# Hybrid encoder layer step: two more projection blocks taken from unscaled rows, layer norm's factor and shift applied behind the spatial products, and an instruction order that counts the shared PSUM banks

## The chip, the cores and the metric

The kernel runs on one NeuronCore of a Trainium2 chip, in fp32. The metric is the device time of one execution in microseconds (us), as a median of runs. Engines are named as in the profile: PE (matrix products), PEld (its weight loads), DVE, ACT and POOL (elementwise work), SP (which issues most DMAs). A bank is one of the eight PSUM banks into which PE writes.

## What is computed

One layer of a streaming encoder on 576 tokens: 64 of a running stream and 512 of a new one, width 1024. Cut to what matters:

```python
h   = rms_norm(x) * g
p   = h @ w_in                    # columns r|k|v|lora w,a,g | u|gv | gate_A | gate_B
o_A = rwkv7(p[r,k,v,lora])        # token shift, decay, delta rule state per head
vn  = layer_norm(p[gv])           # (gv - mean) * rstd * ln_v_g + ln_v_b
z   = einsum('gts,bnsgc->bntgc', w_spatial * tril, vn) + b_spatial
o_B = p[u] * z
m   = sigmoid(p[gate_A]) * (o_A @ w_proj_a) + sigmoid(p[gate_B]) * (o_B @ w_proj_b)
x   = x + rms_norm(m @ w_o)
x   = x + rms_norm(swiglu(rms_norm(x)))
```

The normalised `vn` of the 64 running tokens is an output too. The token shift is `p + (p_prev - p) * mu`. The recurrence is done in chunks of 64 tokens: per chunk a 64 x 64 triangular inverse, then a short chain of states over nine chunks.

## The kernel before

**Layout.** Channels lie on partitions and the 576 tokens along the free dimension, in two halves of 288. A projection *block* is 128 output channels: for eight input tiles, two halves and three terms, 48 matmuls of 128 x 288. Three terms, because every fp32 operand is split into a rounded part and a rest (`hi`, `lo`), and hi*hi, hi*lo and lo*hi are added. A weight block is loaded (`wraw`, L280, two buffers), split by ACT (`whi`, L287) and POOL (`wlo`, two halves, L290) into three buffers.

**Start.** x is loaded and multiplied by the norm's gain; its split is `u0..u7` (the unscaled rows: the factor 1/rms of each token is missing). From these come the two lora blocks (`pfw`, `pfg`), then k and r of the first head pair (`pk`, L546 to L560), which are kept in `st` tiles. The token factors `rs0` are ready meanwhile, and `Shifted(scale=True)` (L465) multiplies such a block by them before the token shift (L468 to L473). The scaled and split rows `h0..h7` (L583, L331, L332) follow; all later blocks use them (`pj`). Then the early pool `xpool` is closed and its space is given to the pools of the head pairs.

**Weave.** The order of PE's instructions is written out by a planner, class `Weave`: PE executes exactly in that order. There are streams, written as Python generators, and background blocks:

- `elementwise` of each of eight head pairs: z (lora products), n (norms of k), am (products within chunks; twice two banks, then two), tb and tr (transposes), tv (transposes of v), wv, bo;
- `inverse` of each pair: m1, m2, mp, mu, d, e and c, y, in this order, behind the small inverse on DVE (X, M, with DMAs through `d_inv`);
- `chain` (states, pc, then py), `finish` (group norm, to, g, store to `d_oa`);
- behind the pairs: layer norm (`ln_all`), spatial products z (`ob_all`), loading of `d_oa` (`oa_all`), norms.

A stream hands control back with a number, after which it may go on, or with an event and a number. The numbers are the estimates in `LAT`: n2 from k to n, tb between transposes, e0 ahead of e and so on; `name@p` holds for pair p alone. The planner keeps a clock `now`, raised by each matmul's estimated time. When no stream may go on it takes three more matmuls of the current block. If the estimate is short, PE stands at that instruction and waits; if it is long, the stream goes on late and blocks run in between.

Blocks wait in a list: first `F0` gate blocks, then for each pair its k, r, v (which need the event A of the pair before; pair 0 has only v here) and `FILL[p]` more gate and u blocks (`spill`, stored to `d_ga`, `d_gb`, `d_u`), then the four gv quarters, then the three blocks that are left. A block whose need isn't there yet is passed over for a later one.

**Banks.** During the pairs four banks with tag `a` are shared by all streams (`ps1`), three serve blocks, one the state chain. They are given in turn. The planner doesn't know of them: PE waits at a matmul whose bank hasn't been read out.

**Other engines.** The orders of DVE, ACT, POOL and SP are set at build time by a scheduler with its own estimates, in priority of the program's order, and are fixed too.

**Layer norm.** Per group of rows (one of 64, four of 128 tokens): statistics, then ACT applies mean and 1/sigma (L1099), POOL multiplies by the gain and DVE adds the shift, each in two halves of 512 (L1102, L1103). Gain and shift lie in slots 5 and 6, broadcast to 128 partitions by DMA (L1017). In `ob_all`, eight groups g of 128 channels are multiplied by the masked `wsT` (name z, L1129), and the bias is added on DVE (L1132, L1133).

Of the kernel before, what the change touches and what calls it, by code (L numbers as in the profile page):

```python
# [5 lines left out]
F32 = mybir.dt.float32  # L6
# [6 lines left out]
P = 128  # L13
# [24 lines left out]
FILL = (1, 0, 2, 6, 3, 3, 1, 2)  # L38
LAT = {
# [4 lines left out]

# [37 lines left out]
def host_layout(a):  # L82
# [49 lines left out]
class Weave:  # L132
# [89 lines left out]
def layer(tc, I, O):  # L222
# [27 lines left out]
    ps1 = lambda name: psum.tile([P, 512], F32, tag="a", bufs=nb["a"], name=name)  # L250
# [278 lines left out]
    with tc.manual_schedule(engines={mybir.EngineType.PE}):  # L529
# [103 lines left out]
    def elementwise(E):  # L633
# [38 lines left out]
        s = ps1("n2")[:, 0:10].rearrange("p (j h) -> p j h", h=2)  # L672
# [34 lines left out]
        banks = lambda: [ps1("am").rearrange("p (j t) -> p j t", t=P) for _ in range(2)]  # L707
# [20 lines left out]
        yield LAT["am"]  # L728
        pm = banks()
# [729 lines left out]
```

## Time and profile before

| | us |
|---|---|
| median of 3 runs (lowest, highest) | 1274.91 (1273.36, 1278.71) |
| the profiled execution | 1273.24 |
| its span, first to last instruction | 1271.5 |
| PE busy | 1195.4 (94%) |
| DVE, ACT, POOL busy | 583.3, 466.2, 630.5 |
| mean granted PE clock | 0.968 |

The span is what the profiler saw between the first and the last instruction. Busy time of PE overstates its work a little, since matmuls overlap. A time in square brackets behind an instruction is how long its engine stood idle ahead of it, with the instruction that ended the wait. "DMA issue" rows give the size and the time from issue to landing. The granted clock is the share of full speed that the chip allowed PE.

### The profile page before, as it was taken

The page shows a single profiled execution, that of the slowest core. Times are in us where ns is not written, and L with a number is a line of the kernel's source. Part 1 is how long each engine was busy: PE and PEld are TensorE (multiplying, and loading weights), DVE is VectorE, ACT ScalarE, POOL GpSimd, SP SyncE. Part 2 cuts the span into 40 slices and gives each one's busy share as a digit, 9 for nine tenths or more (in the row PEclk, how much of TensorE's full clock was granted, in tenths as well). Part 3 has the DMA queues.
Part 4 walks back from the last instruction along what each step waited for, and adds up shares of the span by engine and source line. Part 5 has one row for each costly group of instructions (what it writes and reads, how often), then busy time and mean ns, then how long its engine had stood idle before and what let it go on. Part 6 is the DMA issues. An engine that isn't in the chain of part 4 may idle for free.

```text
span 1271.5 us, 29927 instructions
## 1 busy us (share of the span) xinstructions
PE 1195.4 (94%) x12922; PEld 1162.5 (91%) x12922; DVE 583.3 (46%) x1077; ACT 466.2 (37%) x887; POOL 630.5 (50%) x492
## 2 busy tenths in 40 slices
PE   7889999999999989999879999989999999999997
PEld 6789888888898889899879999989999999999997
DVE  5965576663656647562741542464333333310003
ACT  5634343535253544443431233452222222222220
POOL 6554253533445344542663654366565656544442
PEclk8898899899899999999889999989999999999998
DMA  5212222223131313132554543223222222242222
GB/s 178 81 58 75 58 80 61 76 69 103 41 105 56 86 57 100 52 112 71 157 161 130 179 138 117 69 108 90 82 84 84 84 84 82 85 158 82 84 76 75
DMA packets 68404, 118.56 MB, mean 93 GB/s; under 512 B 30832, under 2 KB 36208, under 8 KB 68272
## 3 DMA queue, kind: packets, MB, share of 16 engines
q1 hardware_dynamic: 68128, 116.58, 30.3%
q8 instruction: 101, 1.65, 0.6%
q14 instruction: 31, 0.25, 0.1%
q10 hardware_dynamic: 144, 0.07, 0.0%
HBM read 100.35 MB, written 16.28 MB: 92 GB/s over the span
## 4 chain that ended last, share of the span: by engine, by line
PE 68%; DVE 15%; ACT 5%; POOL 4%; issue 4%; DMA 3%; SPq 1%; DVEq 0%; POOLq 0%; ACTq 0%
PE fg L271 20%; PE po L271 14%; PE pj L271 11%; PE pb L271 4%; PE pa L271 4%; PE gv L271 3%; POOL wlo L290 2%; DVE X L828 2%; PE am L271 1%; DVE Xt L825 1%; PE fp L271 1%; SPq L833 1%; PE z L271 1%; PE pc L271 1%; DVE L L650 1%
## 5 line engine op out<-in xcount | busy, mean ns | idle before, releaser
L290 POOL TENSOR_TENSOR wlo<-raw,whi 128x512 fp32r<-128x512 f32 (+1 forms) x288 | 406.5, 1434 | 372.4 <-ACT whi L287 352.5
L287 ACT ACTIVATE whi<-raw 128x1024 fp32r<-128x1024 f32 x144 | 150.2, 1046 | 283.9 <-PE fg L271 172.2
L1209 DVE TENSOR_TENSOR rs<-rs,nsq 128x288 f32<-128x288 f32 (+2 forms) x12 | 9.0, 754 | 104.7 <-ACT nsq L1208 104.7
L1277 DVE TENSOR_TENSOR ft<-ft,fg 128x288 f32<-128x288 f32 x40 | 16.4, 451 | 67.1 <-PE fg L271 65.5
L1271 DVE TENSOR_TENSOR fg<-fg,rs 128x288 f32<-128x288 f32 x40 | 16.4, 453 | 62.3 <-PE fg L271 62.2
L828 DVE TENSOR_TENSOR X<-X,Xt 80x15 f32<-80x15 f32 (+7 forms) x120 | 42.4, 353 | 3.4
L825 DVE TENSOR_TENSOR Xt<-X,M 80x15 f32<-80x15 f32 (+7 forms) x120 | 37.6, 314 | 8.7 <-DMA M<-d_inv 5.4
L976 POOL TENSOR_TENSOR gm<-gm,mhalf 128x10 f32<-128x10 f32 x8 | 16.2, 2023 | 42.8 <-DVE gm L975 42.8
L1274 DVE SCALAR_TENSOR_TENSOR ft<-ft,fg 128x576 f32<-128x576 f32 (+1 forms) x24 | 28.4, 1183 | 19.3 <-ACT ft L1273 19.3
L740 POOL TENSOR_TENSOR BK<-BK,EL 128x576 f32<-128x576 f32 x16 | 18.7, 1171 | 36.1 <-PE am L271 36.1
L1275 POOL TENSOR_TENSOR ft<-ft,rs 128x576 f32<-128x576 f32 (+1 forms) x24 | 31.8, 1326 | 7.1 <-DVE ft L1274 7.1
L271 PE MATMUL pj<-h0h,wlo 128*128 128x288 f32 x92 | 28.2, 307 | 5.7 <-POOL wlo L290 5.7
L836 DVE STREAM_TRANSPOSE IT<-IV 128x640 f32<-128x640 f32 x16 | 13.5, 841 | 43.9 <-DMA IV<-d_inv 31.1
L668 POOL TENSOR_TENSOR aq<-aq,k 128x576 f32<-128x576 f32 x8 | 12.8, 1604 | 39.4 <-DVE k L473 27.8
L271 PE MATMUL pj<-h0h,whi 128*128 128x288 f32 x92 | 29.8, 324 | 2.3 <-ACT whi L287 2.3
L271 PE MATMUL pj<-h4l,whi 128*128 128x288 f32 x92 | 28.0, 305 | 3.5 <-DVE h4l L332 3.5
L271 PE MATMUL pj<-h3h,whi 128*128 128x288 f32 x92 | 29.8, 324 | 0.0
L271 PE MATMUL pj<-h2h,whi 128*128 128x288 f32 x92 | 29.7, 323 | 0.0
L271 PE MATMUL pj<-h1h,whi 128*128 128x288 f32 x92 | 29.6, 321 | 0.0
L271 PE MATMUL pj<-h4h,whi 128*128 128x288 f32 x92 | 29.4, 319 | 0.0
L271 PE MATMUL pj<-h7h,whi 128*128 128x288 f32 x92 | 29.3, 319 | 0.0
L271 PE MATMUL pj<-h5h,whi 128*128 128x288 f32 x92 | 29.0, 316 | 0.0
(1194 smaller groups left out, 4309.4 us busy)
## 6 DMA issues: line engine op xcount, KB each, us to landing
raw<-in_w_in SPq DMA_DIRECT2D x50, 512.0 KB, 3.7
raw<-in_w_gate SPq DMA_DIRECT2D x22, 512.0 KB, 3.6
raw<-in_w_up SPq DMA_DIRECT2D x22, 512.0 KB, 3.6
raw<-in_w_down SPq DMA_DIRECT2D x16, 512.0 KB, 3.5
raw<-in_w_gv SPq DMA_DIRECT2D x8, 512.0 KB, 3.6
raw<-in_w_proj_a SPq DMA_DIRECT2D x8, 512.0 KB, 4.0
raw<-in_w_proj_b SPq DMA_DIRECT2D x8, 512.0 KB, 3.6
raw<-in_w_o SPq DMA_DIRECT2D x8, 512.0 KB, 3.6
```

The costliest lines, as they stand in the source:

```text
L271: return pe.matmul(out, lhsT, rhs, **kw)
L287: keep(act.activation(hi[:, :cols], raw[:, :cols], ACT.Copy))
L290: keep(pool.tensor_tensor(lo[:, c0:c1], raw[:, c0:c1], f(hi[:, c0:c1]), ALU.subtract))
L740: pool.tensor_tensor(by_chunk(BK[:, x, :]), by_chunk(BK[:, x, :]), EL[:, :, 64:65].broadcast_to([P, NCH, 64]), ALU.mult)
L825: ins = dve.tensor_tensor(t3, X[:, 0:r, s:s + 1].broadcast_to([NU, r, w]), M[:, s:s + 1, s + 1:SB].broadcast_to([NU, r, w]), ALU.mult)
L828: dve.tensor_tensor(X[:, 0:r, s + 1:SB], X[:, 0:r, s + 1:SB], t3, ALU.add)
L836: turn = lambda: dve.transpose(IT.rearrange("p c t -> p (c t)"), IV.rearrange("p c t -> p (c t)"))
L976: pool.tensor_tensor(m, m, mhalf, ALU.pow)
L1271: keep(dve.tensor_tensor(g[:, HS[h]], pg, rs2[:, HS[h]], ALU.mult))
L1274: keep(dve.scalar_tensor_tensor(t[:, ts], t[:, ts], 1.0, g[:, ts], ALU.add, ALU.mult))
L1275: pool.tensor_tensor(t[:, ts], t[:, ts], rs2[:, ts], ALU.mult)
L1277: dve.tensor_tensor(t[:, HS[h]], t[:, HS[h]], pu, ALU.mult)
```

## The change

1. **Start.** Behind k and r of pair 0, its v and the first gate_A block are also computed from the unscaled rows. v waits in an `st` tile (now three) and is scaled with the others. The gate block is multiplied by `rs0` on DVE, goes through Tanh on ACT, and is stored from a tile of `xpool`. Both blocks leave the weave's list, and `FILL` of pair 3 falls from 6 to 5.
2. **Order.** `Weave` counts the four shared banks: a request gives the time for which it holds the bank (`take`), and a stream that needs n banks hands control back until n are free by that count (`free(n)`). Every `ps1` of the pairs gets such a pair of lines; not all are shown. Many estimates in `LAT` change, e0 counts from d and not from the values, and AB is transposed last of three.
3. **Layer norm.** Gain and shift are applied to the 64 running tokens only. For the other four groups the gain, constant along a channel, is multiplied behind the spatial product, and the shift becomes `ln_b[c] * sum_s(w[t,s]) + b_spatial[t]`: two products of ones with `wsT` and eight DVE operations compute this once, into slot 5.

```diff
-FILL = (1, 0, 2, 6, 3, 3, 1, 2)
+FILL = (1, 0, 2, 5, 3, 3, 1, 2)
 LAT = {
-    "z0": 5.4, "z": 0.85, "n2": 4.9, "n2t": 0.4, "am0": 3.7, "am": 1.6, "tb0": 3.5, "tb": 0.8, "tv0": 4.6, "tv": 1.3, "bo0": 3.5, "bo": 0.4,
-    "last": 0.4, "ln": 3.5, "oa": 3.9, "oaj": 0.15, "z1": 18.0, "zz": 1.5, "rs": 2.15, "rb": 2.8, "f": 1.1, "f0": 1.0, "sq": 0.44,
-    "M": 5.5, "U": 20.0, "m1": 2.3, "m2": 2.4, "mp": 3.3, "mu": 2.0, "d0": 2.2, "e0": 2.3, "y0": 3.5,
-    "ch0": 2.6, "S": 1.5, "y": 0.5, "gn1": 4.0, "gn2": 6.0, "to": 3.5, "to1": 0.45, "g": 1.8,
-
-    "am0@0": 6.4, "am0@1": 5.6, "n2@0": 1.4, "tb0@1": 2.9, "M@0": 3.4,
+    "z0": 5.4, "z": 0.85, "n2": 6.2, "n2t": 0.4, "am0": 3.7, "am": 2.0, "tb0": 3.5, "tb": 1.3, "tv0": 5.2, "tv": 1.3, "bo0": 3.5, "bo": 0.4,
+    "last": 0.4, "ln": 3.5, "oa": 3.9, "oaj": 1.2, "z1": 15.0, "zs": 3.0, "zz": 1.5, "rs": 2.15, "rb": 2.8, "f": 1.1, "f0": 1.0, "sq": 0.44,
+    "M": 5.5, "U": 20.3, "m1": 2.3, "m2": 2.4, "mp": 4.2, "mu": 2.0, "d0": 2.2, "e0": 3.1, "y0": 3.5,
+    "ch0": 3.4, "S": 1.6, "y": 0.5, "gn1": 4.0, "gn2": 6.0, "to": 3.5, "to1": 0.45, "g": 1.8,
+
+    "am0@0": 6.4, "am0@1": 5.6, "n2@0": 4.2, "n2@1": 7.2, "n2@3": 7.2, "tb0@1": 3.5, "M@0": 3.4,
 }
...
+    def take(self, hold):
+
+        self.banks.sort()
+        self.banks.pop(0)
+        self.banks.append(self.now + hold)
+
+    def free(self, n=1):
+
+        while sorted(self.banks)[n - 1] > self.now:
+            yield sorted(self.banks)[n - 1] - self.now
...
-    ps1 = lambda name: psum.tile([P, 512], F32, tag="a", bufs=nb["a"], name=name)
+    def ps1(name, hold=0.0):
+        clk.take(hold)
+        return psum.tile([P, 512], F32, tag="a", bufs=nb["a"], name=name)
...
-        kr = []
-        for h in range(4):
...
+        raw0 = {}
+        for nm, b in (("k", BLK_K), ("r", BLK_R), ("v", BLK_V), (None, BLK_GA)):
+            w = wf[2] if nm == "k" else wblock(I["w_in"][b])
+            st = xp.tile([P, T], F32, name="st0") if nm is None else wp.tile([P, T], F32, tag="st", bufs=3, name="st")
+            for h in range(2):
+                ps = pk if (nm, h) == ("k", 0) else [psd("pk")[:, 0:HALF]] * 2
+                for k in range(2 if (nm, h) == ("k", 0) else 0, KD):
+                    mm(ps, w, uh, ul, k, KD, halves=(h,))
+                if (nm, h) == (None, 1):
+                    clk.prepare()
+                if nm is None:
+                    dve.tensor_tensor(st[:, HS[h]], ps[0], rs0[:, HS[h]], ALU.mult)
+                    act.activation(st[:, HS[h]], st[:, HS[h]], ACT.Tanh, scale=0.5)
+                else:
+                    act.activation(st[:, HS[h]], ps[0], ACT.Copy)
+            if nm is None:
+                sp.dma_start(d_ga[0], st)
+            raw0[nm] = st
...
-        s = ps1("n2")[:, 0:10].rearrange("p (j h) -> p j h", h=2)
+        yield from clk.free()
+        s = ps1("n2", 1.6)[:, 0:10].rearrange("p (j h) -> p j h", h=2)
...
-        banks = lambda: [ps1("am").rearrange("p (j t) -> p j t", t=P) for _ in range(2)]
+        banks = lambda: [ps1("am", 3.0).rearrange("p (j t) -> p j t", t=P) for _ in range(2)]
+        yield from clk.free(4)
         pm = banks()
...
-        rest = ps1("tr").rearrange("p (j v) -> p j v", v=P)
-        for i, (dst, src) in enumerate(((AB, BK[:, 0, :]), (At, AR[:, 0, :]), (Kt, BK[:, 1, :]))):
-            pt = ps1("tb").rearrange("p (j v) -> p j v", v=P)
+        yield from clk.free(2)
+        rest = ps1("tr", 5.0).rearrange("p (j v) -> p j v", v=P)
+        for i, (dst, src) in enumerate(((At, AR[:, 0, :]), (Kt, BK[:, 1, :]), (AB, BK[:, 0, :]))):
+            yield from clk.free()
+            pt = ps1("tb", 1.5).rearrange("p (j v) -> p j v", v=P)
...
-        pp = [ps1("d").rearrange("p (u t) -> p u t", t=P) for _ in range(3)]
+        yield from clk.free(3)
+        pp = [ps1("d", 2.8).rearrange("p (u t) -> p u t", t=P) for _ in range(3)]
...
-        yield (("values", hp_), LAT["e0"])
+        yield LAT["e0"]
+        yield (("values", hp_), 0.0)
...
-        pe_ = [ps1("e").rearrange("p (j a t) -> p j a t", a=2, t=64) for _ in range(2)]
-        pq = [ps1("c") for _ in range(2)]
+        yield from clk.free(4)
+        pe_ = [ps1("e", 4.0).rearrange("p (j a t) -> p j a t", a=2, t=64) for _ in range(2)]
+        pq = [ps1("c", 4.2) for _ in range(2)]
...
-        py = [ps1("y").rearrange("p (u v) -> p u v", v=HD) for _ in range(3)]
+        yield from clk.free(3)
+        py = [ps1("y", 3.2).rearrange("p (u v) -> p u v", v=HD) for _ in range(3)]
...
-            sp.dma_start(R["ln"][i], I["rows"][i:i + 1, :].broadcast_to([P, D]))
+            sp.dma_start(R["ln"][i][0:64], I["rows"][i:i + 1, :].broadcast_to([64, D]))
...
-            for i in range(2):
-                cs = slice(i * 512, (i + 1) * 512)
-                pool.tensor_tensor(vn[0:n, cs], vn[0:n, cs], gain[0:n, cs], ALU.mult)
-                dve.tensor_tensor(vn[0:n, cs], vn[0:n, cs], shift[0:n, cs], ALU.add)
             if n == 64:
+                for i in range(2):
+                    cs = slice(i * 512, (i + 1) * 512)
+                    pool.tensor_tensor(vn[0:n, cs], vn[0:n, cs], gain[0:n, cs], ALU.mult)
+                    dve.tensor_tensor(vn[0:n, cs], vn[0:n, cs], shift[0:n, cs], ALU.add)
                 sp.dma_start(O["vn_s"], vn[0:64])
...
+        pb = R["ln"][0]
+        for i in range(2):
+            ps = psum.tile([P, 512], F32, tag="h", bufs=6, name="zs")
+            mmul(ps, one.broadcast_to([P, P]), R["wsT"][:, i * 512:(i + 1) * 512], start=True, stop=True)
+            for g in range(4 * i, 4 * i + 4):
+                gs = slice(g * P, (g + 1) * P)
+                dve.scalar_tensor_tensor(pb[:, gs], ps[:, (g % 4) * P:(g % 4 + 1) * P], V("ln_b", g), R["bias"][:, gs], ALU.mult, ALU.add)
+        yield LAT["zs"]
...
-            dve.tensor_tensor(zb[:, 64:T].rearrange("p (c t) -> p c t", t=P), pz[1].rearrange("p (c t) -> p c t", t=P),
-                              bs.unsqueeze(1).broadcast_to([P, 4, P]), ALU.add)
+            dve.scalar_tensor_tensor(zb[:, 64:T].rearrange("p (c t) -> p c t", t=P), pz[1].rearrange("p (c t) -> p c t", t=P), V("ln_g", g),
+                                     pb[:, gs].unsqueeze(1).broadcast_to([P, 4, P]), ALU.mult, ALU.add)
...
-        for nm, b, x_ in (("k", BLK_K, kr[0]), ("r", BLK_R, kr[1])):
+        for nm, b in (("k", BLK_K), ("r", BLK_R), ("v", BLK_V)):
             take = Shifted(b, nm, scale=True)
-            EV[0][nm] = [take(h, x_[:, HS[h]]) for h in range(2)][1]
-        clk.signal("k", 0)
-        clk.signal("r", 0)
+            EV[0][nm] = [take(h, raw0[nm][:, HS[h]]) for h in range(2)][1]
+            clk.signal(nm, 0)
```

More of the change, by code (lines that the diff above doesn't have):

```diff
@@ L769, in elementwise @@
         v = E["v"]
-        pvs = [ps1("tv").rearrange("p (j v) -> p j v", v=P) for _ in range(2)]
+        yield from clk.free(2)
+        pvs = [ps1("tv", 1.6).rearrange("p (j v) -> p j v", v=P) for _ in range(2)]
         for j in range(5):
@@ L781, in elementwise @@
         WV = rp.tile([P, 10, HD], F32, tag="WV", name="WV")
-        pw = [ps1("wv").rearrange("p (u v) -> p u v", v=HD) for _ in range(2)]
+        yield from clk.free(2)
+        pw = [ps1("wv", 2.4).rearrange("p (u v) -> p u v", v=HD) for _ in range(2)]
         for c, j, half_ in PLACES:
@@ L801, in elementwise @@
         for hs in HS:
-            sb = ps1("bo")
+            yield from clk.free()
+            sb = ps1("bo", 1.2)
             mmul(sb[:, 0:HALF], bonesr, rkh[:, hs], start=True, stop=False)
@@ L842, in inverse @@
         yield lat("m1", hp_)
-        pp = ps1("m1")[:, 0:10 * SB].rearrange("p (c t) -> p c t", t=SB)
+        yield from clk.free()
+        pp = ps1("m1", 1.8)[:, 0:10 * SB].rearrange("p (c t) -> p c t", t=SB)
         for u in range(10):
@@ L848, in inverse @@
         yield lat("m2", hp_)
-        pp = ps1("m2")[:, 0:10 * SB].rearrange("p (c t) -> p c t", t=SB)
+        yield from clk.free()
+        pp = ps1("m2", 2.2)[:, 0:10 * SB].rearrange("p (c t) -> p c t", t=SB)
         for u in range(10):
@@ L858, in inverse @@
         yield lat("mp", hp_)
-        pp = ps1("mp")[:, 0:320].rearrange("p (c t) -> p c t", t=32)
+        yield from clk.free()
+        pp = ps1("mp", 1.9)[:, 0:320].rearrange("p (c t) -> p c t", t=32)
         for u in range(10):
@@ L865, in inverse @@
         yield lat("mu", hp_)
-        pp = ps1("mu")[:, 0:320].rearrange("p (c t) -> p c t", t=32)
+        yield from clk.free()
+        pp = ps1("mu", 1.9)[:, 0:320].rearrange("p (c t) -> p c t", t=32)
         for u in range(10):
@@ L952, in chain @@
         Y = E["Y"]
-        py = [ps1("py")[:, 0:320].rearrange("p (j v) -> p j v", v=HD) for _ in range(2)]
+        yield from clk.free(2)
+        py = [ps1("py", 2.2)[:, 0:320].rearrange("p (j v) -> p j v", v=HD) for _ in range(2)]
         for c, j, half_ in PLACES2:
@@ L982, in finish @@
         for js, t0, t1 in (((0, 2, 1, 3), 0, START2[4]), ((4,), START2[4], T)):
-            pt = ps1("to")
+            yield from clk.free()
+            pt = ps1("to", 1.4)
             for j in js:
@@ L990, in finish @@
         for hs in HS:
-            ps = ps1("g")
+            yield from clk.free()
+            ps = ps1("g", 1.4)
             for n, (w, xx) in enumerate(((lh, dgh), (lh, dgl), (ll, dgh))):
```

35 lines of the change are left out of this document (13 added, 22 removed).

## The prediction

> **What bounds the kernel now.** I read the page's busy shares and 40 slices first, then a table by stage, then the PE timeline with its waits.
>
> ```profile
> PE 1195.4 (94%) x12922; PEld 1162.5 (91%) x12922; DVE 583.3 (46%) x1077; ACT 466.2 (37%) x887; POOL 630.5 (50%) x492
> ...
> PE   7889999999999989999879999989999999999997
> ...
> PEclk8898899899899999999889999989999999999998
> ```
>
> PE is busy 94% of 1271.5 us; no other engine passes half. Its losses lie in the left half, and there the granted clock dips too. So the question is how many of PE's lost microseconds the change gives back. By stage (columns: us, then busy time and count of PE, PEld, DVE, ACT, POOL, granted clock, DMA):
>
> ```profile
> 42.40:76.40 34.00, 25.26 (x149) 23.66 (x147) 27.12 (x25) 17.89 (x37) 23.02 (x18) 0.85 0.21 70
> 76.40:552.80 476.40, 443.40 (x6918) 420.84 (x6916) 285.75 (x627) 210.92 (x481) 215.64 (x171) 0.96 0.26 74
> 552.80:603.50 50.70, 49.95 (x840) 48.32 (x839) 16.19 (x41) 17.22 (x38) 14.17 (x11) 1.00 0.29 88
> 603.50:660.00 56.50, 46.03 (x332) 44.41 (x332) 37.76 (x52) 22.07 (x35) 38.20 (x27) 0.88 0.49 152
> 660.00:723.00 63.00, 62.56 (x463) 60.49 (x464) 18.86 (x37) 12.96 (x16) 32.80 (x24) 1.00 0.48 141
> 723.00:1271.50 548.50, 535.23 (x4017) 532.83 (x4016) 168.38 (x264) 159.83 (x238) 283.50 (x215) 0.99 0.31 96
> 975.00:1000.00 25.00, 25.00 (x191) 25.00 (x190) 8.00 (x13) 6.96 (x8) 14.62 (x11) 1.00 0.28 85
> ```
>
> The last row is PE unhindered: 25.00/191 = 0.131 us for a matmul, so 6.3 us for a 48-matmul block. Three stages lose time: the start of the weave (8.7 us idle, clock 0.85), the eight head pairs (33.0 us idle, clock 0.96: 4% of 476.4 = 19 us withheld) and the layer norm (10.5 us idle, clock 0.88: 12% of 56.5 = 6.8 us withheld). What follows 723 is not touched.
>
> PE need not be the bound of the pairs merely because it is busy: they hang on a chain (inverse, then state). These rows tell:
>
> ```profile
> 143.29 1.66 PE y L271 x75
> ...
> 536.34 1.66 PE y L271 x75
> ...
> 589.09 1.66 PE y L271 x75
> ```
>
> From y of the first pair to y of the last is 445.8 us, 63.7 a pair. The last interval, with no later pair's elementwise work beside it, took 52.8: that is the chain's own length. So a pair is some 11 us longer than its chain, and fill blocks on PE set it. After the last pair's state PE still owes projection work:
>
> ```profile
> 602.92 0.57 PE L271 MATMUL py<-S,AR 64*64 64x64 f32 x26
> ```
>
> ```profile
> 632.30 0.38 ACT L433 ACTIVATE s<-gv 128x256 f32<-128x256 f32 x1 [2.34 <-PE gv L271]
> ```
>
> The chain ends at 603.5, the gv block at 632: PE is 28 us behind the chain. PE work removed or moved forward shortens the span until that is used up.
>
> **Part 1: two more raw blocks.** Today PE finishes the k and r blocks of the unscaled rows at 42.4, and then takes the gate block from the scaled rows, which aren't ready.
>
> ```profile
> 50.05 0.40 PE L271 MATMUL pj<-h4l,whi 128*128 128x288 f32 x1 [3.52 <-DVE h4l L332]
> ...
> 54.38 0.44 PE L271 MATMUL pj<-h0h,wlo 128*128 128x288 f32 x1
> ...
> 66.84 1.29 PE L271 MATMUL n<-cst,q 128*128 128x2 f32 x10 [2.84 <-ACT q L664]
> ```
>
> From 42.4 to 76.4 there are 149 records: 131 block matmuls (17.2 us at 0.131), 8 of z (1.0), 10 of n (1.3). 34 us held 19.5 us of work; 14.5 were lost. After the change v and the first gate block (2 x 6.3 us) run from 42.4 to 55.1 on the rows that k and r have used already. The scaled rows are there by 54.4 (PE is then in the second half of its block and has used each of them), so they stall nothing after 55.1. The weight splits find room:
>
> ```profile
> 43.43 5.96 POOL L290 TENSOR_TENSOR wlo<-raw,whi 128x512 fp32r<-128x512 f32 x4 [5.29 <-ACT whi L287]
> ```
>
> POOL needs 3.0 us for a block and stood idle for 5.3 before these two, waiting for weight buffers that the new order frees in the same way. Gone from the loss are the 3.5 and its neighbours; the n wait stays. I expect it to grow, since the first pair's own chain starts when the early pool is given back:
>
> ```profile
> 54.27 0.76 DVE L332 TENSOR_TENSOR dgl<-tg,dgh 128x576 fp32r<-128x576 f32 x1 [0.75 <-ACT dgh L331]
> 55.17 1.91 DVE L465 TENSOR_TENSOR k<-st,rs 128x288 f32<-128x288 f32 x2
> ```
>
> ```profile
> 55.13 0.34 SPq L818 DMA_DIRECT2D X<-in_cst  x1
> ```
>
> A DMA into an unrelated new tile and the scaling of k both begin as dgl ends at 55.03, so the new pools wait for the last user of the old one. The new gate tile st0 lies in that pool and is stored from it:
>
> ```profile
> d_ga<-st SPq DMA_DIRECT2D x1, 288.0 KB, 2.1
> ```
>
> PE ends its block at 55.1, multiply and Tanh take about 1, the store 2.1: the chain starts near 58.5 in place of 55.2, behind the gate's store in SP's queue, and v's scaling (another 1.9 as for k) and shift stand in DVE's queue before the scan of L. The larger n2@0 can't help: n follows z0 (5.4) and four z steps, already past 4.2. So n waits some 3 to 5 us and about 1.5 more go to a low clock: a loss of 6 in place of 14.5, **-8**. Bounds: n waiting for the whole 3.3 + 2.9 more on top of 2.84 leaves -3; only the 2.84 left, -12. In the pair itself v is there early, so the token transposes no longer wait for a block; that gives the chain its 3 us back. If the fill that hides it were missing, the late chain would cost 3.5.
>
> **Part 2: the order.** PE's waits inside the pairs (total, times, longest):
>
> ```profile
> PE e L271 <- ACT AB L882: 4.7, 7, 0.7
> PE n L271 <- ACT q L664: 4.1, 2, 2.1
> PE mp L271 <- DVE IT L836: 3.9, 2, 2.3
> PE tr L275 <- DVE AB L757: 3.5, 2, 2.1
> ...
> PE am L271 <- DVE AR L909: 2.4, 3, 0.8
> PE tv L275 <- DVE Y L958: 2.3, 1, 2.3
> PE pc L271 <- DVE S L946: 1.5, 2, 1.2
> ...
> PE n L271 <- DVE AR L909: 1.1, 1, 1.1
> PE py L271 <- DVE AB L718: 1.1, 2, 0.8
> PE d L271 <- DVE AB L718: 1.1, 2, 0.7
> ```
>
> Each has its edit: e0 now counts from d (4.7), n2 rises (4.1), mp 3.3 to 4.2 (3.9), AB is transposed last and tb rises (3.5), S 1.5 to 1.6 (1.5); am, tv, py, d and the second n stood on a shared bank that its last reader had not emptied (8.0), which the count now foresees. Together 25.7 us. What fills these places is projection blocks that must run anyway. The cost: steps come later on the chain, up to 2.4 at e (3.1 against the 0.7 it really needs), 0.9 at mp, 0.3 at U, and 1.5 at tb in the elementwise work, so a chain of 52.8 becomes about 57, still below 63.7 less what PE gains. A step delayed that way holds up only its own stream. Between 0 and 25.7 I take half, since estimates that fit one order fit the next only partly: **-13**. Of the withheld 19 us I take a quarter, **-5** (bounds 0 and 12).
>
> The Trainium skill, "TensorE: Matmul & The Clock Gate" (Part 1), has the clock halved only after an idle window of about 3.4 us. By it, gaps of 2 us cost no clock and closing them returns none; the sum would be 7 higher. The trace is split:
>
> ```profile
> 76.00:108.00 32.00, 29.91 (x316) 28.77 (x315) 14.64 (x43) 11.21 (x29) 14.48 (x14) 1.00 0.31 84
> 108.00:125.00 17.00, 14.98 (x273) 14.29 (x272) 11.30 (x15) 10.59 (x23) 9.29 (x7) 0.80 0.24 70
> ```
>
> The first stage holds the 2.1 us gap of tr and kept its clock, the second a 2.0 us gap of n and lost a fifth of it.
>
> **Part 3: layer norm.** Gain and shift leave four of five row groups: 8 of 10 multiplies on POOL and 8 adds on DVE.
>
> ```profile
> L1102 POOL TENSOR_TENSOR s<-s,s x10: 1264/1288/2402, 626.7 to 654.8; 128x512 f32<-128x512 f32 x8, 64x512 f32<-64x512 f32 x2
> ```
>
> ```profile
> 646.54 0.40 PE L271 MATMUL pj<-h0h,whi 128*128 128x288 f32 x1 [1.53 <-ACT whi L287]
> 651.94 0.61 PE L271 MATMUL pj<-h0h,wlo 128*128 128x288 f32 x1 [4.87 <-POOL wlo L290]
> ```
>
> 8 x 1.29 = 10.3 us leave POOL just where a weight split stood behind two pairs of them while PE waited 4.87. Of 6.4 us I take 5 (ACT's normalising, 1.2 us a group, stays in front of the other) and 2 of the withheld 6.8: **-7** (bounds -2, -11).
>
> **Part 4: what is added.** Two fp32 products of 512 columns. A z group is 64 + 4 x 128 = 576 columns:
>
> ```profile
> 698.26 1.45 PE z L271 x10
> ```
>
> so 1024 columns cost 1.45/576 x 1024 = **+2.6** on PE. Eight DVE operations of 128 columns from PSUM, about 0.3 each, lie beside pa products, where DVE is busy 19 of 63 us; z is placed at 15 + 3 for 18 before, and the one-pass multiply-add replaces an add of equal shape.
>
> **Sum:** -8 - 13 - 5 - 7 + 2.6 = -30.4. The profiled execution took 1273.24 (span 1271.5), which gives 1242.8; the median of the runs lies 1.7 above it: **1244.5, say 1244**.
>
> **Rivals.** (a) The clock stays as it is: a rule of 3.4 us of idle, gaps of 2 us don't matter; -30.4 + 7 gives 1251. For it the stage to 108, against it the stage behind it. Chance 0.10. (b) The estimates miss again and waits move elsewhere: only -8 - 7 + 2.6 = -12.4, 1262. Chance 0.20: the present waits came from such estimates. (c) Nearly all goes: -10 - 25.7 - 12 - 7 + 2.6 = -52, 1223; chance 0.13. (d) Slower: the counted banks starve the wide steps. am and e now wait until all four banks count as free, d and y for three, while transposes hold a counted bank 5.0 us. If that adds b to each chain, the pair is 57 + b; it decides from 57 + b = 63.7 + (12/7), b = 8.4; at b = 10 it is 7 x 3.3 - 12 = +11, 1286. Against it: the longest bank wait PE saw is 2.3. Chance 0.05. (e) No gain: late chain and longer steps eat the start, 1268 to 1281; chance 0.06.
>
> **How the numbers follow.** Main case 0.46, its own range 1234 to 1257. About 0.5% (6.4 us) is what a measurement here can tell from none. Faster: 0.46 + 0.10 + 0.20 + 0.13 = 0.89; same 0.06; slower 0.05. The range reaches half into (c) and through (b): 1224 to 1266.
>
> **What would show it.** Part 1: no PE wait on h4l, raw blocks to 55, v's transposes right behind the others, n waiting over 3. Part 2: e, tr, am, tv gone from the PE waits and the sum of waits between 76 and gv near 20 in place of 33, clock 0.97. If a step stalls for ACT or DVE as long as before, (b) holds; if PE has gaps before am or e with all blocks done, (d). Part 3: no wlo wait over 2 us behind gv. Wrong would be chiefly: the state of the last pair ending no earlier than PE's gv blocks.

## The result and the profile after

The changed kernel takes **1255.07 us** (median of 4 runs, 1251.97 to 1257.89) against 1274.22 for the kernel before on the same chip (4 runs, 1273.36 to 1278.71): a ratio of 0.984, 95% interval 0.981 to 0.988. Timed again with the experiments (5 runs), it took 1257.78 against 1276.84: 0.985, interval 0.983 to 0.987. So it is faster by 19 to 20 us, two thirds of the forecast 30.4, inside the range (1224 to 1266) and inside the main case's own range (1234 to 1257).

The profiled execution took 1257.89 (span 1256.1), the highest of its four, and that of before 1273.24 was the lowest of its own: the two spans differ by 15.4 us where the medians differ by 19. Up to the first product that the change doesn't touch (723.0 and 704.5 us) they differ by 18.5. What follows accounts for the 15.4.

The page of the changed kernel, busy shares and 40 slices:

```profile
PE 1194.0 (95%) x12926; PEld 1159.7 (92%) x12926; DVE 545.3 (43%) x1081; ACT 464.7 (37%) x889; POOL 621.2 (49%) x484
...
PE   6999999998979898889999999899999999999997
...
PEclk8989999998989999999999999999999999999998
```

PE's busy time is about the same as before (1195.4), so most of what was gained is idle time. PE's row no longer dips in slices 2 to 4; now it dips in slices 10 to 18 (some 280 to 565 us). The stages, cut at the same events as before, and then two halves of the weave (us, then busy time and count of PE, PEld, DVE, ACT, POOL, granted clock, DMA):

```profile
42.40:76.40 34.00, 29.30 (x204) 28.69 (x203) 23.90 (x35) 19.34 (x45) 17.23 (x17) 0.94 0.26 84
76.40:616.60 540.20, 508.60 (x7882) 482.22 (x7882) 293.42 (x692) 234.77 (x530) 243.59 (x186) 0.97 0.27 79
616.60:639.50 22.90, 20.70 (x153) 20.01 (x151) 10.79 (x19) 11.85 (x18) 12.62 (x11) 1.00 0.44 136
639.50:704.50 65.00, 64.69 (x469) 61.47 (x470) 19.77 (x44) 12.59 (x15) 34.14 (x26) 1.00 0.46 143
704.50:1256.10 551.60, 537.83 (x4016) 535.49 (x4014) 168.57 (x264) 160.27 (x239) 284.06 (x215) 0.99 0.31 96
76.40:300.00 223.60, 220.32 (x3281) 210.08 (x3280) 126.44 (x301) 102.36 (x235) 109.16 (x88) 0.99 0.28 82
300.00:605.00 305.00, 276.94 (x4507) 260.97 (x4508) 155.88 (x372) 126.47 (x285) 127.02 (x95) 0.95 0.24 68
```

The kernel before, the whole weave and the same halves:

```profile
76.40:632.10 555.70, 518.21 (x7943) 493.10 (x7942) 321.03 (x695) 240.69 (x539) 247.39 (x193) 0.96 0.28 80
76.40:300.00 223.60, 208.74 (x3204) 198.46 (x3203) 136.25 (x301) 98.44 (x226) 98.95 (x81) 0.95 0.26 72
300.00:605.00 305.00, 286.11 (x4566) 272.20 (x4565) 167.04 (x369) 129.91 (x295) 130.86 (x100) 0.98 0.27 78
```

| stage | forecast | measured | how |
|---|---|---|---|
| start, 42.4 to 76.4 | -8 | -7.2 | 204 - 149 = 55 records x 0.131 us |
| weave, to the end of gv | -18 (waits 13, clock 5) | -8.2 | end of gv 632.0 to 616.6 (-15.4), less the start's 7.2 |
| end of gv to the first pa | -7 | -5.3 | 28.2 (from 632.0) to 22.9 |
| pa and z products | +2.6 | +2.2 | 62.8 to 65.0 |
| untouched rest | 0 | +3.1 | 548.5 to 551.6 |
| sum | -30.4 | -15.4 | |

The weave is the row that missed, and by more than it shows. From 76.4 to 605 us the idle time fell only from 33.7 to 31.3 us, at a clock of 0.97 both times. The rest came behind 605, where before the gv blocks waited 3.8 us for their weights: from there to the end of gv PE idled 3.8 us at a clock of 0.87 before, and 0.3 us at 1.00 after. The forecast had priced these waits in none of its terms.

Within the pairs, the first half is what the forecast wanted: 3.3 us idle where there were 14.9, clock 0.99. The second half is worse than before: 28.1 us idle where there were 18.9, clock 0.95 where it was 0.98. PE's largest waits from 76 to 600 us (total, times, longest), after:

```profile
PE n L287 <- ACT q L685: 13.7, 4, 5.9
PE pc L287 <- DVE S L983: 4.1, 7, 1.1
PE am L287 <- DVE oo L1034: 3.6, 2, 2.8
```

The waits at e, mp, tr, tv, py, d and those of am on AR (19.0 of the forecast's 25.7) are gone. But all waits together are 31.1 us in place of 33.4, since **n** now waits 13.7. Its longest waits, PE timeline (start, duration, instruction, idle time ahead of it); the first of them lies ahead of 76:

```profile
72.19 1.01 PE L287 MATMUL n<-cst,q 128*128 128x2 f32 x4 [3.10 <-ACT q L685]
...
303.60 1.64 PE L287 MATMUL n<-cst,q 128*128 128x2 f32 x9 [3.73 <-ACT q L685]
...
370.00 1.23 PE L287 MATMUL n<-cst,q 128*128 128x2 f32 x5 [5.89 <-ACT q L685]
...
434.97 1.23 PE L287 MATMUL n<-cst,q 128*128 128x2 f32 x5 [3.73 <-ACT q L685]
```

Three of these stand in the second half, and the clock falls behind each. Here are 15 us around each of the three:

```profile
299.00:314.00 15.00, 11.27 (x161) 10.54 (x161) 11.10 (x13) 7.11 (x12) 13.14 (x9) 0.77 0.16 45
363.00:378.00 15.00, 9.11 (x124) 8.66 (x123) 10.96 (x12) 7.44 (x15) 12.03 (x8) 0.77 0.16 42
430.00:445.00 15.00, 11.27 (x165) 10.67 (x164) 11.12 (x13) 6.28 (x11) 13.19 (x8) 0.77 0.14 37
```

That is 13.4 us of waiting and 0.23 x 45 = 10.4 us of withheld clock: by this estimate 24 us lost at three instructions, in a half where the kernel before nowhere waited for q. The second profile of the same kernel (e9, below) repeats it: n waits 13.8 us, and the clock of that half is 0.94.

**Why n waits.** n multiplies q. ACT computes q from k alone, but writes it into the one buffer that L has (both have the tag `L` in the kernel). So q has to wait until ACT has read L for the last time (`sg<-L`), L comes from a scan on DVE, and the scan follows z. The planner lets n go n2 (6.2) behind the event of *k*. Here is pair 5, first in the kernel before: z's first product, ACT's last reading of L, q, and n.

```profile
367.98 0.29 PE L271 MATMUL z<-dwr,lwh 128*128 128x288 f32 x1
...
375.66 0.67 ACT L656 ACTIVATE sg<-L 128x576 f32<-128x576 f32 x1
...
385.44 0.78 ACT L664 ACTIVATE q<-k,vec 128x576 f32<-128x576 f32 x1 [0.59 <-DVE k L473]
...
389.46 1.28 PE L271 MATMUL n<-cst,q 128*128 128x2 f32 x10
```

After:

```profile
357.22 0.40 PE L287 MATMUL z<-dwr,lwh 128*128 128x288 f32 x1 [0.88 <-DVE Y L996]
...
367.78 0.67 ACT L677 ACTIVATE sg<-L 128x576 f32<-128x576 f32 x1
...
369.17 0.78 ACT L685 ACTIVATE q<-k,vec 128x576 f32<-128x576 f32 x1
```

Before, k came so late that 21.5 us lay between z and n. L was free 8.4 us behind z (376.33), q waited for k, and n found q ready. After, k is finished at 352.96, ahead of z, and L is free at 368.45. n stands 12.8 us behind z (370.00 - 357.22), and 5.9 of them are waited for. DVE in that stretch of the changed kernel:

```profile
364.14 0.84 DVE L865 STREAM_TRANSPOSE IT<-IV 128x640 f32<-128x640 f32 x1 [4.18 <-DMA IV<-d_inv]
...
365.80 1.35 DVE L671 TENSOR_TENSOR_SCAN L<-rmask,sg 128x576 f32<-128x576 f32 x1
```

DVE's fixed order has the transposition of the inverse of pair 4 ahead of this scan; it waits 4.2 us for its DMA, and the scan stands behind it. Since k was there 16 us ahead of q, a buffer of its own for q would take L and the scan out of n's way as far as the data go. No run tries it, and ACT's fixed order could still hold q back.

### The profile page after: what moved, and what is told of

The parts are those of the page before. It is cut to its first block, busy times and chain, and to the rows that moved or that the text cites. A ratio compares the mean times of both kernels' runs of the same rounds, so it can differ in the third digit from the quotient of the medians.

```text
span 1256.1 us, 29917 instructions
## 1 busy us (share of the span) xinstructions
PE 1194.0 (95%) x12926; PEld 1159.7 (92%) x12926; DVE 545.3 (43%) x1081; ACT 464.7 (37%) x889; POOL 621.2 (49%) x484
## 4 chain that ended last, share of the span: by engine, by line
PE 75%; DVE 12%; issue 3%; DMA 3%; ACT 3%; POOL 2%; SPq 1%; DVEq 0%; ACTq 0%; POOLq 0%
PE fg L287 20%; PE pj L287 16%; PE po L287 15%; PE pb L287 4%; PE pa L287 4%; PE gv L287 3%; DVE Xt L854 2%; DVE X L857 2%; PE am L287 1%; PE z L287 1%; PE y L287 1%; PE d L287 1%; SPq L862 1%; PE c L287 1%; PE n L287 1%
## 5 line engine op out<-in xcount | busy, mean ns | idle before, releaser
L306 POOL TENSOR_TENSOR wlo<-raw,whi 128x512 fp32r<-128x512 f32 (+1 forms) x288 | 401.7, 1418 | 397.2 <-ACT whi L303 350.1
L1014 POOL TENSOR_TENSOR gm<-gm,mhalf 128x10 f32<-128x10 f32 x8 | 19.6, 2450 | 63.3 <-DVE gm L1013 52.1
L944 DVE TENSOR_TENSOR TD<-e,AR 64x256 f32<-64x256 f32 x32 | 13.4, 419 | 68.4 <-PE e L287 68.2
L983 DVE TENSOR_TENSOR S<-pc,C 128x64 f32<-128x64 f32 x48 | 10.6, 221 | 66.1 <-PE pc L287 58.6
L854 DVE TENSOR_TENSOR Xt<-X,M 80x15 f32<-80x15 f32 (+7 forms) x120 | 34.7, 290 | 6.9 <-DMA M<-d_inv 3.7
L857 DVE TENSOR_TENSOR X<-X,Xt 80x15 f32<-80x15 f32 (+7 forms) x120 | 30.8, 257 | 3.3
L287 PEld LDWEIGHTS n<-cst,q 128*128 128x128 f32 x80 | 13.2, 252 | 18.1 <-ACT q L685 18.0
L287 PE MATMUL n<-cst,q 128*128 128x2 f32 x80 | 13.7, 297 | 16.8 <-ACT q L685 16.8
L287 PE MATMUL am<-AR,BK 64*64 64x128 f32 x640 | 24.4, 280 | 4.9 <-DVE oo L1034 3.6
L287 PE MATMUL pj<-h0h,whi 128*128 128x288 f32 x88 | 28.2, 320 | 0.4 <-ACT st L433 0.4
L287 PE MATMUL pj<-h6h,whi 128*128 128x288 f32 x88 | 28.5, 323 | 0.0
```

The lines of the kernel that those rows point to most:

```text
L287: return pe.matmul(out, lhsT, rhs, **kw)
L306: keep(pool.tensor_tensor(lo[:, c0:c1], raw[:, c0:c1], f(hi[:, c0:c1]), ALU.subtract))
L854: ins = dve.tensor_tensor(t3, X[:, 0:r, s:s + 1].broadcast_to([NU, r, w]), M[:, s:s + 1, s + 1:SB].broadcast_to([NU, r, w]), ALU.mult)
L857: dve.tensor_tensor(X[:, 0:r, s + 1:SB], X[:, 0:r, s + 1:SB], t3, ALU.add)
L944: dve.tensor_tensor(TD[rows, cs, rows], ps[rows, :, 1, :], by_place[rows, cs, 0, :], ALU.add)
L1014: pool.tensor_tensor(m, m, mhalf, ALU.pow)
```

## The experiments

All leave the computation whole. Each ratio is to the kernel before in the same series of runs.

**Each part alone.** e1 has part 1 (with `FILL[3]` at 5) on the kernel before, e2 part 2, e3 part 3.

e1, core of the edit (the loop is the one shown with the change):

```diff
-FILL = (1, 0, 2, 6, 3, 3, 1, 2)
+FILL = (1, 0, 2, 5, 3, 3, 1, 2)
...
+        for nm, b in (("k", BLK_K), ("r", BLK_R), ("v", BLK_V), (None, BLK_GA)):
```

e2 (the estimates of the change except z1 and zs, `take` and `free`, AB last):

```diff
+    "M": 5.5, "U": 20.3, "m1": 2.3, "m2": 2.4, "mp": 4.2, "mu": 2.0, "d0": 2.2, "e0": 3.1, "y0": 3.5,
...
+        yield from clk.free()
+        s = ps1("n2", 1.6)[:, 0:10].rearrange("p (j h) -> p j h", h=2)
```

e3 (gain and shift behind the products, z1 15.0 and zs 3.0):

```diff
+            dve.scalar_tensor_tensor(zb[:, 64:T].rearrange("p (c t) -> p c t", t=P), pz[1].rearrange("p (c t) -> p c t", t=P), V("ln_g", g),
+                                     pb[:, gs].unsqueeze(1).broadcast_to([P, 4, P]), ALU.mult, ALU.add)
```

> The kernel before with part 1 alone: v and the first gate block of pair 0 from unscaled rows, FILL of pair 3 at 5, old estimates, no count of banks, layer norm as before. Theory A (PE's lost time adds up, the parts are independent): the 55 more matmuls that PE had done by 76.4 us in the changed kernel are 7 us, so 7 us faster (about 1267), and the first chain some 5 us later without cost. Rival B (the new estimates and the start only work together): the old estimates no longer fit, new waits appear, gain under 3 us.

> The kernel before with part 2 alone: the count of the banks, the new estimates, AB transposed last, e0 counted from d. Theory A: 8 us faster (about 1266): the waits on e, tr, tv and shared banks, 25 us of PE, are gone, but waits of n on ACT's q2 of some 14 us take their place. Rival B: the new waits of n come from the changed start (pairs 4 to 6 reached sooner), so without it the order gains 15 us or more and n waits under 5 us.

> The kernel before with part 3 alone: gain and shift behind the spatial products. Theory A: 5.3 us less between the last gv block and the first pa product, 1.9 us more for the two products, so 3 to 4 us faster (about 1271), the wait of pj on POOL's wlo (4.9) gone. Rival B: the wait moves to ACT's whi or to DMA, and only the 1.9 us remain: 2 us slower.

| | median us | ratio | interval | us to before |
|---|---|---|---|---|
| e1, start | 1253.83 | 0.983 | 0.981 to 0.985 | -21.4 |
| e2, order | 1270.48 | 0.996 | 0.994 to 0.998 | -4.7 |
| e3, layer norm | 1267.25 | 0.994 | 0.992 to 0.996 | -8.0 |

The parts alone add to 34 us, together they give 19 to 20. Part 1 is worth nearly three times its forecast. Stages of e1:

```profile
42.40:76.40 34.00, 29.26 (x207) 28.64 (x206) 23.91 (x34) 18.96 (x44) 18.21 (x16) 0.95 0.28 84
...
76.40:613.70 537.30, 504.87 (x7876) 480.45 (x7875) 317.03 (x694) 237.94 (x533) 246.12 (x191) 0.97 0.28 81
```

The start stage does 207 - 149 = 58 records more, 7.6 us, as forecast. The weave is 18.4 us shorter than before (537.3 for 555.7): those 7.6 and nearly 11 more that I hadn't counted. Its idle time is 32.4 us where before had 37.5 (555.70 - 518.21), and the clock rose by a point, some 5 us. Which of its instructions that comes from I can't say: the order of the whole weave shifts when two blocks leave its list. In e2 waits of n take the place of those removed (60 to 640 us; the kernel before has 6.9 there, the change 16.8):

```profile
PE n L286 <- ACT q L681: 12.8, 4, 5.0
```

In e3 the stage behind gv is 8.4 us shorter (28.1 to 19.7 us), with the clock at 1.00. Only the stage is compared: the profiled execution of e3, 1275.44, was the slowest of its ten.

```profile
637.10:656.80 19.70, 19.22 (x146) 18.99 (x144) 4.76 (x14) 9.69 (x15) 9.20 (x9) 1.00 0.73 212
```

Before, the same stage:

```profile
632.10:660.20 28.10, 21.20 (x147) 20.50 (x145) 18.67 (x25) 9.72 (x15) 20.63 (x16) 0.88 0.46 138
```

**Parts 1 and 3 without the order (e5)**, and the change timed again beside it (e9):

> Parts 1 and 3 without part 2: old estimates, no count. Theory A (start and norm add, the new order brings nothing on top of the start): -21 and -7 from the single runs less some overlap, 1246 to 1250, so 5 to 9 us faster than the whole change. Rival B (the new order is worth its 5 us on top): 1258 to 1262, slower than the whole change.

> The changed kernel as it is, timed beside the next three on one chip. All theories: 1253 to 1257; the stage behind the pa products, which the change doesn't touch, shows how far PE's own pace differs from run to run (551.6 us in the first profile of it, 548.5 before, 544.5 to 552.2 in four others).

e5: 1248.53, 0.978 (0.975 to 0.981), -28.3 us, about the sum of e1 and e3 (29.4). e9: 1257.78, 0.985. So in the company of the other two **part 2 costs 9 us**, and that the parts don't add up is its doing. Here is e5, second half of the weave:

```profile
300.00:605.00 305.00, 288.19 (x4599) 274.17 (x4599) 179.04 (x390) 136.00 (x303) 140.17 (x106) 0.98 0.30 86
```

Its waits sum to 30.6 us between 76 and 600, as in the change (31.1). But they are spread over both halves and short (e: 8 times, 0.7 at most; none over 2.4), and the clock stays at 0.98. In the second half e5 idles 16.8 us, the change 28.1 at 0.95. So it isn't the sum of the waits that differs but the clock, which points at the long stalls as what costs.

**The order in its two halves.** e4 is the change with a count that never holds a stream back; e8 is the change with the old estimates.

e4, of the changed kernel:

```diff
-        while sorted(self.banks)[n - 1] > self.now:
-            yield sorted(self.banks)[n - 1] - self.now
+        return
+        yield
```

e8, of the changed kernel (one line of five; all of `LAT` but z1 and zs goes back):

```diff
-    "M": 5.5, "U": 20.3, "m1": 2.3, "m2": 2.4, "mp": 4.2, "mu": 2.0, "d0": 2.2, "e0": 3.1, "y0": 3.5,
+    "M": 5.5, "U": 20.0, "m1": 2.3, "m2": 2.4, "mp": 3.3, "mu": 2.0, "d0": 2.2, "e0": 2.3, "y0": 3.5,
```

> The changed kernel with the new estimates, but no stream ever waits for a counted bank. Theory A (the count removes waits on banks): waits of am, tv, n, py, d on a bank's last reader return, 5 to 8 us of PE, so 5 to 8 us slower than the changed kernel (about 1261). Rival B (the count only moves the wait onto the chain): within 2 us of the changed kernel. Rival C: the count delays steps, without it 3 us or more faster.

> The whole change, count of banks and order of AB included, but with the estimates of before (z1 and zs as changed; e0 2.3 from d). Theory A (it is the larger estimates that shift n ahead of q2; the count itself is harmless): waits of n under 8 us in all, about 1246 to 1250, as without part 2. Rival B (the count by itself lengthens the chain and costs): 1255 or more. Rival C (count and old estimates together are better than either): below 1243.

With parts 1 and 3 present in all of them:

| order | ratio to before | interval |
|---|---|---|
| as before (e5) | 0.978 | 0.975 to 0.981 |
| count, old estimates (e8) | 0.982 | 0.980 to 0.984 |
| new estimates, no count (e4) | 0.990 | 0.987 to 0.993 |
| both (the change, e9) | 0.985 | 0.983 to 0.987 |
| both, n later in three pairs (e6, below) | 0.977 | 0.974 to 0.979 |

The count helps the new estimates by about 7 us. With the old ones it costs about 5, where the two intervals just touch. My theory of under 8 us of n waits in e8 fell (60 to 640 us, where the change has 16.8):

```profile
PE n L287 <- ACT q L685: 25.1, 8, 4.9
```

n waits in e4 too, 12.9 us, and 7.4 in e5. So either half of part 2 brings n early. But e8 has more waits of n than the change and isn't slower (0.982 against 0.985, the intervals overlap): the sum of n's waits alone doesn't put these kernels in order.

**n alone (e6).** The change, with n2 raised in the pairs where n waited most.

```diff
-    "am0@0": 6.4, "am0@1": 5.6, "n2@0": 4.2, "n2@1": 7.2, "n2@3": 7.2, "tb0@1": 3.5, "M@0": 3.4,
+    "am0@0": 6.4, "am0@1": 5.6, "n2@0": 4.2, "n2@1": 7.2, "n2@3": 7.2, "n2@4": 10.0, "n2@5": 12.2, "n2@6": 10.0, "tb0@1": 3.5, "M@0": 3.4,
```

> The whole change with n2 of pairs 4, 5 and 6 at 10.0, 12.2 and 10.0 in place of 6.2, so that PE takes blocks where it now waits 3.7, 5.9 and 3.7 us for q2. Theory A (PE's lost time bounds, what fills a wait is gained): 13 us of waits and some 3 us of low clock less, 8 to 14 us faster than the whole change (about 1243). Rival B (the chain bounds the pairs by now, the wait turns up elsewhere): within 3 us of it.

1246.84, ratio 0.977 (0.974 to 0.979): **11 us below the change**, by three numbers. The three n's go through without a wait (the next one, in pair 7, waits 3.3). First and last of the three:

```profile
303.17 1.28 PE L287 MATMUL n<-cst,q 128*128 128x2 f32 x10
...
425.40 1.28 PE L287 MATMUL n<-cst,q 128*128 128x2 f32 x10
```

and the second half regains what it had lost, 283.91 us busy for 276.94:

```profile
300.00:605.00 305.00, 283.91 (x4574) 267.66 (x4573) 166.44 (x384) 129.81 (x293) 130.97 (x98) 0.96 0.27 80
```

All waits from 76 to 600 are 24.2 us. Not all of the 11 us is n's: the profiles of e9 and e6 differ by 13.3 us, of which 8.1 lie ahead of the products that no part touches and 5.2 within them (551.4 and 546.2, see the end). So the early n's are shown to cost 8 to 11 us, which is what part 2 costs. That doesn't make part 2 a gain: e6 and e5 agree within their intervals. In e6 the first half idles 3.6 us where e5 idles 14.5, but its second half still idles 21.1 at a clock of 0.96 where e5 has 16.8 at 0.98. Why the forecast 18 us don't appear even with n mended stays open.

**The transposition ahead of the scan (e7).** The change, with scan and first transposition held in the program's order on DVE.

```diff
-        dve.tensor_tensor_scan(L.rearrange("p c t -> p (c t)"), rmask.rearrange("p c t -> p (c t)"), sgf, 0.0,
-                               ALU.mult, ALU.add)
+        tc.keep_in_program_order(dve.tensor_tensor_scan(L.rearrange("p c t -> p (c t)"), rmask.rearrange("p c t -> p (c t)"), sgf, 0.0,
+                                                        ALU.mult, ALU.add))
...
-        turn()
+        tc.keep_in_program_order(turn())
```

> The whole change with one DVE order pinned: the scan of L of the next pair stands ahead of the first transposition of the inverse, which waits up to 4.2 us for its DMA. Theory A (q2 is late because the scan stands behind that wait): the scan of pair 5 starts near 362 in place of 365.8, the waits of n on q2 in pairs 4 to 6 fall by 2 to 4 us each, 5 to 10 us faster than the whole change. Rival B (q2 is late for another reason, k's shift or ACT): the waits of n stay over 3 us, time within 3 us.

1264.35, 0.990 (0.988 to 0.993): 6.6 us slower than e9. DVE of e7 in pair 5, where z begins at 359.69:

```profile
365.75 0.52 DVE L490 SCALAR_TENSOR_TENSOR r<-pj,omm,q 128x288 f32<-128x288 f32 x1 [1.50 <-ACT q L488]
368.13 2.41 DVE L671 TENSOR_TENSOR_SCAN L<-rmask,sg 128x576 f32<-128x576 f32 x1
```

The transposition is behind the scan now, yet the scan starts 8.4 us behind z where it was 8.6 (365.80 - 357.22): group norm and the shift of r, which waits 1.5 us for ACT, have come ahead of it. n waited 26.3 us in this run (60 to 640; 16.9 in e9). So the DMA is not the only thing that holds the scan, and whether q could be had earlier at all stays open.

**The gate's store at the start (e10, e11).** e10 is the change with the gate block ahead of v, so that its store leaves `xpool` earlier; e11 adds that to later n's (`n2@4` 13.0, `@5` 12.2, `@6` 10.0).

```diff
-        for nm, b in (("k", BLK_K), ("r", BLK_R), ("v", BLK_V), (None, BLK_GA)):
+        for nm, b in (("k", BLK_K), ("r", BLK_R), (None, BLK_GA), ("v", BLK_V)):
...
-                if (nm, h) == (None, 1):
+                if (nm, h) == ("v", 1):
```

> The whole change with the gate block taken from the unscaled rows before v, not behind it, so that its store out of the early pool lies beside v's matmuls. Theory A (the first pair's chain waits for that store: DVE stood 3.3 us for it, k's scaling began at 61.3): k's scaling begins near 58, the wait of n at 72 (3.1) goes, 3 to 5 us faster than the whole change. Rival B (the chain is late for PE's blocks alone): k's scaling still after 60, no difference.

> Both remedies together: n2 of pairs 4, 5 and 6 at 13.0, 12.2 and 10.0, and the gate block before v. Theory A (they are separate losses of PE): 3 to 5 us below the kernel with the later n alone, about 1241 to 1244, waits of n under 2 us. Rival B (the chain bounds by now): 1246 as before.

e10: 1259.64, 0.987 (0.986 to 0.989), no gain. First the scaling of k, then the scan of L on DVE in the change:

```profile
61.29 0.82 DVE L482 TENSOR_TENSOR k<-st,rs 128x288 f32<-128x288 f32 x2 [3.29 <-DMA d_ga<-st]
...
67.71 1.35 DVE L671 TENSOR_TENSOR_SCAN L<-rmask,sg 128x576 f32<-128x576 f32 x1
```

and in e10:

```profile
56.18 2.14 DVE L482 TENSOR_TENSOR k<-st,rs 128x288 f32<-128x288 f32 x2 [2.72 <-ACT whi L303]
58.24 3.00 DVE L482 TENSOR_TENSOR r<-st,rs 128x288 f32<-128x288 f32 x2
...
67.96 1.34 DVE L671 TENSOR_TENSOR_SCAN L<-rmask,sg 128x576 f32<-128x576 f32 x1
```

The store's wait is real and e10 removes it: k is scaled 5.1 us earlier. The scan comes no earlier, nor does n (71.99, waiting 3.99). DVE's order changed with the edit: the scalings of k and r take 3.5 us longer (see the end), and v's shift (65.85, 2.18 us) now stands ahead of the scan, where in the change it stands behind it. So taking the store's wait away is not enough to start the first pair's chain earlier; whether it would be with the rest of DVE's order kept was not tried. e11: 1244.88, 0.976 (0.974 to 0.979), the same as e6; its first n still waits 4.0.

**All n's late (e12).** The change with n2 raised in pairs 0 and 4 to 7 (14.5, 13.0, 12.2, 10.0, 7.2).

```diff
-    "am0@0": 6.4, "am0@1": 5.6, "n2@0": 4.2, "n2@1": 7.2, "n2@3": 7.2, "tb0@1": 3.5, "M@0": 3.4,
+    "am0@0": 6.4, "am0@1": 5.6, "n2@0": 14.5, "n2@1": 7.2, "n2@3": 7.2, "n2@4": 13.0, "n2@5": 12.2, "n2@6": 10.0, "n2@7": 7.2, "tb0@1": 3.5, "M@0": 3.4,
```

> The whole change with n2 of pairs 0, 4, 5, 6 and 7 at 14.5, 13.0, 12.2, 10.0 and 7.2: every wait of n on q2 that the profiles of the change showed is given to blocks, the first pair's 3.1 at 72 included. Theory A (PE's lost time bounds): n waits under 2 us in all, 3 to 6 us below the kernel with the later n of pairs 4 to 6, about 1242. Rival B (the waits move to other steps by now): 1245 to 1249, the sum of PE's waits as there.

1252.73, 0.982 (0.980 to 0.984): 7 us above e6 by the ratios. No n waits on q any longer; the start is the best of all,

```profile
42.40:76.40 34.00, 32.38 (x245) 32.00 (x244) 23.89 (x34) 20.62 (x47) 19.09 (x17) 1.00 0.30 94
```

96 records more than before where the change has 55 more. But the waits of other steps return (60 to 640 us):

```profile
PE pj L287 <- POOL wlo L306: 8.3, 4, 3.6
...
PE wv L287 <- DVE AB L783: 2.8, 1, 2.8
PE g L287 <- ACT oo L1025: 2.7, 3, 1.6
```

Blocks now wait for POOL's split of their weights (in the change once, 1.3), and wv and g for elementwise work. That the gain of the start goes this way is what the rows suggest; it was not tried by itself.

e6 and e11 are faster than the change and than the kernel before: 0.977 and 0.976.

## Why the prediction was right or wrong

That the time fell inside the main case's range is in part luck, since two errors cancel. By the medians, part 1 gave 21 us for a forecast of 8, part 3 with its added products 8 for 4.4, and part 2 lost 9 in company where 18 were forecast.

**What bounds the kernel: held.** The last product of the last state, py, starts at 599.90, and gv ends at 616.6: PE is still 17 us behind the chain, and everything gained on PE ahead of it moved the end.

**Part 1 in its stage: held.** -7.2 for -8; no wait on h4l, and n waits 3.10, over 3 as forecast. Three details fell. The raw blocks end at 57.5, not 55.1, with one wait of 1.6 us on ACT's reading of the bank. And "the chain starts near 58.5, behind the gate's store" is right as a wait (k's scaling stood 3.3 us for it) but taking that wait away moved neither the scan nor n (e10). And the chain did not get 3 us back from the early v: the first y starts at 148.6 where it was at 143.2. What was missing is a term for part 1's effect on the weave: nearly 11 us in e1.

**Part 2: the term that failed.** "Between 0 and 25.7 I take half, -13" and "-5" of clock: the weave gave -8.2 in all, little of it in the pairs, and part 2 in the change is worth +9 (e9 against e5), 27 us from its forecast. Most of the waits listed did go, and the clock of the first half did come back; that half of the reasoning held. The step that failed is the row "n ... 4.1" priced as cured by a larger n2. That price was read off the wait n had in the kernel before, with k as late as it was there. With part 2, k comes earlier, n2 counts from k, and q cannot be written before L has been read, which counts from z. So the wait moved from the steps that were mended to the one whose estimate hangs on the wrong event, and grew to 13.7 plus some 10 of clock. e6 gives 8 to 11 us back; the other 16 to 19 by which part 2 missed have no cause shown here. By the prediction's own sign ("if a step stalls for ACT or DVE as long as before, (b) holds"; sum of waits "near 20", measured 31.1) rival (b)'s mechanism, waits that move elsewhere, holds in the second half of the weave, and the time (1255) lies between the main case (1244) and (b) (1262).

**Rival (a): borne out in part.** That the clock stays as it is was wrong: it moved both ways, 0.95 to 0.99 in the first half, 0.98 to 0.95 in the second. But the three stalls behind the second figure last 3.7 to 5.9 us, longer than the idle time that this rival names, and e5's shorter ones left the clock at 0.98. **Rival (d): its price is not shown.** No stall before am or e with all blocks done was seen; the count costs 5 us with the old estimates and saves 7 with the new, far from the 10 us a pair of that case.

**Part 3: right in kind, a little too large in company and too small alone.** -5.3 for -7; the wlo wait behind gv is 1.27 us where it was 4.87, under 2 as forecast. Alone it gave 8.4 in its stage, with the whole withheld clock back: 0.88 to 1.00, which is 3.4 of this stage's 28.1 us. I had counted 2 of 6.8, a figure for the longer stretch from 603.5.

**Part 4: held.** The four zs records begin at 675.32 and take 1.88 us; the stage grew by 2.2 for 2.6.

**The rest.** +3.1 us where nothing was changed. The second profile of the change shows it too (551.4). The other kernels range from 544.5 to 552.4 for these same products (below), so whether the change has a hand in it stays open.

## What to carry to other kernels

An estimate that orders work should count from the event that the step truly waits for; one that counts from a neighbour holds only while the neighbour is late, and mending other steps takes that cover away. Before a wait is priced as cured, ask what its instruction would wait for if everything else were on time: here it was the buffer of L, free 8.4 us behind z in the trace of before, which was there to be read off. An operand's buffer can hold a step back as much as its data. And a change of several parts is best timed in parts: two of these three did more without the third.

## What the runs showed of the hardware

**A short gap can cost clock too.** Three stretches of e6, 3 us each:

```profile
425.00:428.00 3.00, 2.18 (x68) 1.92 (x57) 1.62 (x3) 3.00 (x6) 1.85 (x2) 1.00 0.02 5
428.00:431.00 3.00, 2.12 (x52) 1.84 (x55) 3.00 (x3) 1.46 (x4) 3.00 (x2) 0.62 0.00 0
431.00:434.00 3.00, 3.00 (x66) 2.69 (x61) 2.66 (x6) 1.18 (x4) 3.00 (x3) 0.50 0.60 166
```

```profile
424.61 0.86 PE L287 MATMUL m<-IT,AB 16*32 16x16 f32 x80
...
428.88 0.61 PE L287 MATMUL g<-dgh,lgh 128*128 128x288 f32 x1 [1.71 <-ACT oo L1025]
```

The only gap there is 1.71 us, and the clock fell to 0.50; ahead of it stand 80 products of 16 columns, n's ten of 2 and three wide ones. The 2.1 us gap of the kernel before at 87, among wide products, kept the clock at 1.00. The Trainium skill ("TensorE: Matmul & The Clock Gate", Part 1) has the clock halved after an idle window of about 3.4 us. Half clock is what the trace shows, and behind the changed kernel's longer stalls too (5.89 us, then 0.50 from 370 to 373), but here after 1.7 us of idle; the measurement decides. That narrow products count as idle for the chip would fit these two gaps; no run here tests it. Nor does the shape of a gap settle it: n waits 1.24 us at 117.30 in e1 and 1.25 us at 117.27 in e8, with the same narrow products on both sides, and from 121.3 to 123.3 the clock is 0.50 in e1 and 1.00 in e8.

**The same products at different paces.** The products behind pa are the same 4015 to 4017 records in every kernel. PE waits only 5 to 6 us there, at a granted clock of 0.98 to 0.99. They took 547.5 to 548.5 us in the profiles without part 3 (before, e1, e2), 551.3 to 552.4 in eight of the eleven with it, and 544.5 (e4), 544.7 (e11) and 546.2 (e6) in the other three: 1.4% between the ends. Only the change has two profiles (551.6 and 551.4), so whether the kernel or the single execution sets the pace is not shown. So of two single profiles a stage is to be compared, not the span.

**DVE beside POOL.** The scaling of k and r took 0.82 us each in the change and 2.14 and 3.00 in e10 (rows above). POOL in the change, and then in e10:

```profile
57.59 3.79 POOL L306 TENSOR_TENSOR wlo<-raw,whi 128x512 fp32r<-128x512 f32 x3
```

```profile
55.26 5.67 POOL L306 TENSOR_TENSOR wlo<-raw,whi 128x512 fp32r<-128x512 f32 x4 [7.20 <-ACT whi L303]
```

In e10 both scalings lie beside POOL's weight splits (55.26 to 60.93); in the change they start as the splits end (61.38). That took 3.5 of the 5.1 us by which e10 began earlier (2.14 + 3.00 against twice 0.82). The Trainium skill ("SBUF — State Buffer", SBUF: two separate sides) says that such a pair of operations of the two engines can't run at once, one blocking the other for its whole length; a split takes 1.4 us, so 0.82 and a wait for one split is near 2.14, and 3.00 lies between one wait and two.
